# First head's key projected ahead of its query, ScalarE issuing two kinds of stores, and the merge's first loads in four buffers at a fixed place

## The chip, the cores and the metric

The kernel runs on one core of a Trainium2 chip. The metric is the device time of one execution in microseconds; the median of three runs of the kernel before is 1483.13 us (1480.83 to 1486.48).

## What is computed

One step of one layer of a streaming encoder, on 1024 new frames (the prompt) and 32 further frames of a running stream (the samples), T = 1056 tokens of D = 1024 channels. Cut to what matters here:

```python
u = rmsnorm(x) @ w_in               # gq gk gv gr gg | dq dk dv dg | ma mb
dq, dk = rope(dq, pos), rope(dk, pos)
o_gla  = gla(gq, gk, gv, log_a)                     # 4 heads, chunks of 64
o_diff = softmax(q1 k1) v - lam * softmax(q2 k2) v  # 8 heads, two halves of 64 each
yg = rmsnorm(o_gla) * silu(gg)
yd = rmsnorm(o_diff) * (1 - lambda_init) * silu(dg)
merged = sigmoid(ma) * (yg @ w_proj_gla) + sigmoid(mb) * (yd @ w_proj_diff)
return x + rmsnorm(merged @ w_out)                  # and new k, new v, new states
```

## The kernel before

**Numbers.** Everything is fp32. A product is made of three matmuls on split operands: high part of the weights by high part of the data, low by high, high by low (`wh`, `wl`; `X` holds both parts of the data). So every operand of TensorE is first split by ScalarE (the rounded copy) and VectorE or GpSimd (the rest).

**Stages.** Norm and value projections (to about 222 us), the four GLA heads (to 560), differential attention with its eight heads (to 1182), the merge: the projection `pg` of yg (to about 1286), `pd` of yd, `w_out`, and the end. The change is in attention and at the start of the merge.

**How the order is made.** TensorE's order is written out by a planner, `class Order`. Several threads (generators) give steps with a cost, with events that they need and a latency after each (table `W`), and with the PSUM banks that they take. At each moment the first thread whose step is ready by the planner's clock goes: ahead of all the attention heads (`diff_main`), then the samples (`sample_thread`), then `fill`. Fill is a list of projection jobs, in the order of `jobs`. One job is 72 matmuls of 128 x 352: three chunks of 352 tokens, each 8 slices of the channels by 3 products. TensorE runs exactly this list (`tc.manual_schedule(engines=PE)`). The order of the other engines is made by the framework's scheduler, which sees the same program; each engine, SP with its DMA issues included, then works in order, and an instruction that waits holds what is behind it.

**Jobs of attention.** For head h there are `dq h`, `dk h` and `dg h` (the silu gate), and between them 16 gate jobs `g` for the merge, whose tanh is stored to DRAM (`thd`, L484). Before: dq 0, g, dk 0, g, dq 1, g, dk 1, dg 0, dq 2, g, dk 2, dg 1, and so on.

**From a dk job to the scores.** ScalarE evacuates the three chunks to `rr` (L806). SP issues four small DMAs that swap rows for the rope (`sw`, L798 and L799); GpSimd multiplies `sw` by a sine table (L800), VectorE multiplies `rr` by a cosine table (L802, three pieces) and adds (L804). Then ScalarE makes `k0` and `k1` in eight pieces (L833, L834) and VectorE the rests `kl0` and `kl1` (L835, L836). Each of the four tiles is needed in both halves of the partitions, so SP issues four DMAs that copy one half to the other (L839), after a store of the new keys (L827). The scores of a block are two pairs of matmuls: `k0` and `kl0` with `q0`, then `k1` and `kl1` with `q1` (L883, L884); the planner lets them start at the end of the job dk plus `W["dk"]` = 14.32 us, and of dq plus `W["dq"]` = 7.76 us. A dq job has the rope too, and splits into `q0` and `q1` without the copies across halves (L813 to L818). There is one set of `k` and `kl` tiles for all heads.

**The end of a head.** The last scores, transposes (L931) and PV products (L944 to L946) of a head are followed by the first scores of the next, and only then by `diff_fin` of the old head: the sums of squares by `ones` (L859), their store `msd` (L862), the gating of `osb` on VectorE (L865) and its store `ydd` (L866).

**The merge.** `load_split` issues the loads of the eight `ygr` tiles (L1066) into three buffers, each split by ScalarE (L1069) and VectorE (L1070) to `y`. `pg_first` runs two output blocks together, slice by slice as the tiles come; the loads of its weights (`wtile`, L429, one buffer `wr` for the raw weights) and of the stored gates `tha` (L1078) are issued where the scheduler puts them.

Of the kernel before, what the change touches and what calls it, by code (L numbers as in the profile page):

```python
# [11 lines left out]
F32 = mybir.dt.float32  # L12
F32R = mybir.dt.float32r
I32 = mybir.dt.int32
AF = mybir.ActivationFunctionType
ALU = mybir.AluOpType
# [4 lines left out]
P = 128  # L21
NP = 1024
NS = 32
T = NP + NS
D = 1024
KT = D // P
PAST = 512
GH, GDV = 4, 256
DH, HD = 8, 64
# [10 lines left out]
BLK_GQ, BLK_GK, BLK_GG, BLK_DQ, BLK_DK, BLK_DG, BLK_MA, BLK_MB = 0, 4, 8, 16, 24, 32, 40, 48  # L40
BLK_PG, BLK_PD = 56, 64
# [81 lines left out]
def hybrid_step_kernel(ctx: ExitStack, tc: tile.TileContext, a):  # L123
    nc = tc.nc
    mm = nc.tensor.matmul
    act = nc.scalar.activation
    ve = nc.vector
    dma = nc.sync.dma_start
    st = nc.sync.dma_start

    def pool(name, bufs=1, **kw):
        return tc.alloc_tile_pool(name=name, bufs=bufs, **kw)
# [296 lines left out]
    def wtile(b):  # L429
        wr = wp.tile([P, KT, P], F32, tag="wr", bufs=1, name="wr")  # L430
        dma(wr, a["w128"][b])
        wh = odd(wp, KT, P, tag="wh", name="wh")
        act(wh, wr, AF.Copy)  # L433
        wl = odd(wp, KT, P, tag="wl", name="wl")
        nc.gpsimd.tensor_tensor(wl, wr, wh.bitcast(F32), op=ALU.subtract)  # L435
        return wh, wl
# [44 lines left out]
    def gate_job(b, w, j):  # L481
        def begin():
            th = rp.tile([P, T], F32, tag="gate", name="gate")
            return (lambda ps, sl: act(th[:, sl], ps, AF.Tanh, scale=0.5)), (lambda: st(thd[w, j], th))  # L484
        return b, ("gate", w, j), begin, []


# [259 lines left out]
    jobs = []  # L747
# [43 lines left out]
    def rot_job(b, event, needs, split):  # L791
        def begin():
            r = dp.tile([P, T], F32, tag="rr", name="rr")

            def done():
                for m in range(2):
                    o = m * HD
                    dma(sw[o : o + 8], r[o + 8 : o + 16])  # L798
                    dma(sw[o + 8 : o + 16], r[o : o + 8])  # L799
                nc.gpsimd.tensor_tensor(sw, sw, stb, op=ALU.mult)  # L800
                for c in parts(T, N["rr"]):
                    ve.tensor_tensor(r[:, c], r[:, c], ct[:, c], op=ALU.mult)  # L802
                for c in parts(T, N["rr"]):
                    ve.tensor_tensor(r[:, c], r[:, c], sw[:, c], op=ALU.add)  # L804
                split(r)
            return (lambda ps, sl: act(r[:, sl], ps, AF.Copy)), done  # L806
        return b, event, begin, needs

    def split_q(h):
        def f(r):  # L810
            q0 = dp.tile([P, NP], F32R, tag=f"q0{h % 2}", name="q0")
            q1 = dp.tile([P, NP], F32R, tag=f"q1{h % 2}", name="q1")
            for c in parts(NP, N["q"]):  # L813
                act(q0[0:64, c], r[0:64, c], AF.Copy, scale=SC)
                act(q1[64:128, c], r[64:128, c], AF.Copy, scale=SC)
                ve.scalar_tensor_tensor(q0[64:128, c], r[0:64, c], SC, q0[0:64, c].bitcast(F32),
                                        op0=ALU.mult, op1=ALU.subtract)
                ve.scalar_tensor_tensor(q1[0:64, c], r[64:128, c], SC, q1[64:128, c].bitcast(F32),  # L818
                                        op0=ALU.mult, op1=ALU.subtract)
            qsam[h] = sam(0, h)  # L820
            act(qsam[h], r[:, NP:T], AF.Copy, scale=SC)
            dqs[h] = q0, q1
        return f

    def split_k(h):
        def f(r):
            st(a["newk"][h], r)  # L827
            k0 = dp.tile([P, NP], F32R, tag="k0", name="k0")
            k1 = dp.tile([P, NP], F32R, tag="k1", name="k1")
            kl0 = dp.tile([P, NP], F32R, tag="kl0", name="kl0")  # L830
            kl1 = dp.tile([P, NP], F32R, tag="kl1", name="kl1")
            for c in parts(NP, N["k"]):
                act(k0[0:64, c], r[0:64, c], AF.Copy)  # L833
                act(k1[64:128, c], r[64:128, c], AF.Copy)  # L834
                ve.tensor_tensor(kl0[0:64, c], r[0:64, c], k0[0:64, c].bitcast(F32), op=ALU.subtract)  # L835
                ve.tensor_tensor(kl1[64:128, c], r[64:128, c], k1[64:128, c].bitcast(F32), op=ALU.subtract)  # L836

            for t, src, dst in ((k0, 0, 64), (k1, 64, 0), (kl0, 0, 64), (kl1, 64, 0)):
                dma(t[dst : dst + 64].bitcast(F32), t[src : src + 64].bitcast(F32))  # L839
            ksam[h] = sam(1, h)  # L840
            act(ksam[h], r[:, NP:T], AF.Copy)
            dks[h] = (k0, k1), (kl0, kl1)
        return f

    def dgate_job(h):
# [6 lines left out]
            return silu_into(dsg[h]), done  # L852
        return BLK_DG + h, ("dg", h), begin, [(("fin", h - 1), 0.0)] if h else []

    def diff_fin(h, osb, sqo):
        for n0 in (0, 512):
            yield 0.86, [(("pv", h, 3), W["pv"])], ["o"]
            ps = obank("ps_m")
            mm(ps, one_h, sqo[:, n0 : n0 + 512], start=True, stop=True)  # L859
            act(sqo[0:1, n0 : n0 + 512], ps[0:1], AF.Copy)  # L860
            S.free("o", W["m_o"])
        st(msd[h : h + 1, :], sqo[0:1, :])  # L862
        yield 0.0, [(("dg", h), 0.0)], []
        for c in parts(NP, N["fin"]):
            ve.scalar_tensor_tensor(osb[:, c], osb[:, c], gs_half, dsg[h][:, c], op0=ALU.mult, op1=ALU.mult)  # L865
        st(ydd[h, :, 0:NP], osb)  # L866
        S.mark(("fin", h))

    def diff_scores(h, i, out):
# [168 lines left out]
    for h in range(-1, DH):  # L1038
        need = [(("qk", h - 1), 0.0)] if h >= 1 else []
        n = GATES_DIFF[h + 1]  # L1040
        if h + 1 < DH:
            jobs.append(rot_job(BLK_DQ + h + 1, ("dq", h + 1), need, split_q(h + 1)))
        jobs += [gate_job(*gates.pop(0)) for _ in range(min(n, 1))]
        if h + 1 < DH:
            jobs.append(rot_job(BLK_DK + h + 1, ("dk", h + 1), need, split_k(h + 1)))
        if h >= 0:
            jobs.append(dgate_job(h))
        jobs += [gate_job(*gates.pop(0)) for _ in range(n - 1)]
# [9 lines left out]
    lp_ = pool("ldp", reuse_waits="tile")  # L1058

    def ld(name):  # L1060
        return lp_.tile([P, T], F32, tag="ld", bufs=3, name=name)

    def load_split(src, dst, stage, scale=lambda k, r: None):
        for k in range(KT):
            r = stage(k)
            dma(r, src[k])  # L1066
            scale(k, r)
            y = dst[k]
            act(y[:, 0, :], r, AF.Copy)  # L1069
            ve.tensor_tensor(y[:, 1, :], r, y[:, 0, :].bitcast(F32), op=ALU.subtract)  # L1070

    load_split(ygd, ytiles, lambda k: ld("ygr"))
    tha = {}

    def load_tha(j):
        if j < KT:
            tha[j] = ld("tha")
            dma(tha[j], thd[0, j])  # L1078
# [5 lines left out]

    def pg_first():

        w = [wtile(BLK_PG + j) for j in range(2)]
        for j in range(2):
            load_tha(j)
        b = []  # L1090
        for j, k in sorted(((j, k) for j in range(2) for k in range(KT)), key=lambda e: (e[1] + N["lead"] * e[0], e[0])):
            yield 1.36, [(("qk", DH - 1), W["yg0"] + W["yg"] * k)], [] if b else ["pj", "pj", "s", "s"]
            if not b:
                d = [dbank("ps_w") for _ in range(2)]
                b = [bank("ps_w"), bank("ps_w")] + [d[n // 2][:, n % 2 * 512 : n % 2 * 512 + 512] for n in range(4)]
            wh, wl = w[j]
            for n, (t0, cw) in enumerate(CHUNKS):
                ps = b[j * 3 + n]
                mm(ps[:, :cw], wh[:, k, :], ytiles[k][:, 0, t0 : t0 + cw], start=(k == 0), stop=False)
                mm(ps[:, :cw], wl[:, k, :], ytiles[k][:, 0, t0 : t0 + cw], start=False, stop=False)  # L1100
                mm(ps[:, :cw], wh[:, k, :], ytiles[k][:, 1, t0 : t0 + cw], start=False, stop=(k == KT - 1))
            if k == KT - 1:
                with tc.high_priority(offset=N["evac"]):
                    for n, (t0, cw) in enumerate(CHUNKS):
                        pg_evac(j)(b[j * 3 + n][:, :cw], slice(t0, t0 + cw))
                st(ptd[j], tha[j])
                load_tha(j + 2)
                for tag in ("pj", "pj") if j == 0 else ("s", "s"):
                    S.free(tag, W["pg_b"])
        yield from fill([pg_job(j) for j in range(2, KT)], ytiles)  # L1110

    def pg_job(j):
# [4 lines left out]
            return pg_evac(j), done  # L1117
        return BLK_PG + j, ("pg", j), begin, []

    with tc.manual_schedule(engines=PE):  # L1120
        S.run(left + [[pg_first(), None, nullcontext]])
    tp.release()
    rp.release()
    cp = pool("cp", side="right", reuse_waits="tile")
# [176 lines left out]
```

## Time and profile before

| | |
|---|---|
| median of 3 runs | 1483.13 us (1480.83 to 1486.48) |
| the profiled execution | 1483.59 us, its span 1481.9 us |
| TensorE busy | 1422.6 us (96%) |
| VectorE, ScalarE, GpSimd busy | 786.6, 601.0, 298.4 us |
| attention with its fill (560 to 1182 us) | 622 us, TensorE busy 604.9 |
| start of the merge (1182 to 1290 us) | 108 us, TensorE busy 102.5 |

The page gives the span, then each engine's busy time with its share and its number of instructions. The waits view lists who waited for whom: total in us, how often, the longest. The timeline has one row for each instruction or for several of a kind: start, duration, engine, line, what it writes and reads, and in brackets the idle time before it and what ended it. The chain of waits goes back from the last instruction and shows DMAs with the time to their landing. In windows, PEclk is the clock that TensorE was granted, 1.00 being full speed. A matmul's duration overlaps with the next one's, so its cost is the distance between two starts.

### The profile page before, as it was taken

The page shows a single profiled execution, that of the slowest core. Times are in us where ns is not written, and L with a number is a line of the kernel's source. Part 1 is how long each engine was busy: PE and PEld are TensorE (multiplying, and loading weights), DVE is VectorE, ACT ScalarE, POOL GpSimd, SP SyncE. Part 2 cuts the span into 40 slices and gives each one's busy share as a digit, 9 for nine tenths or more (in the row PEclk, how much of TensorE's full clock was granted, in tenths as well). Part 3 has the DMA queues.
Part 4 walks back from the last instruction along what each step waited for, and adds up shares of the span by engine and source line. Part 5 has one row for each costly group of instructions (what it writes and reads, how often), then busy time and mean ns, then how long its engine had stood idle before and what let it go on. Part 6 is the DMA issues. An engine that isn't in the chain of part 4 may idle for free.

```text
span 1481.9 us, 22365 instructions
## 1 busy us (share of the span) xinstructions
PE 1422.6 (96%) x8848; PEld 1327.6 (90%) x8848; DVE 786.6 (53%) x1464; ACT 601.0 (41%) x1262; POOL 298.4 (20%) x186
## 2 busy tenths in 40 slices
PE   8999999989999999899999999999899899999997
PEld 6787789889989899899989998998899799999997
DVE  5702005755565343576767767678665535455415
ACT  5612114535344232455555555555455432221311
POOL 1200002222213224123222222222221111122001
PEclk9999999999999999999999999999999999999999
DMA  8621111122222233323232333223322278633205
GB/s 310 205 105 38 45 45 48 56 74 68 81 70 73 70 120 108 90 62 106 72 108 60 106 86 96 69 83 90 92 68 81 97 264 302 223 131 129 103 1 192
DMA packets 66742, 156.58 MB, mean 106 GB/s; under 512 B 10008, under 2 KB 28568, under 8 KB 65600
## 3 DMA queue, kind: packets, MB, share of 16 engines
q1 hardware_dynamic: 66624, 155.01, 32.3%
q8 instruction: 74, 1.21, 0.3%
q14 instruction: 44, 0.36, 0.1%
HBM read 104.39 MB, written 40.04 MB: 97 GB/s over the span
## 4 chain that ended last, share of the span: by engine, by line
PE 51%; DVE 6%; DMA 4%; ACT 2%; issue 1%; POOL 1%; SPq 0%; DVEq 0%; POOLq 0%; ACTq 0%
PE ps_w L465 9%; PE ps_w L466 9%; PE ps_w L467 9%; PE ps_w L444 2%; PE ps_w L443 2%; PE ps_w L445 2%; PE ps_s L884 2%; PE ps_t L931 2%; PE ps_s L883 2%; DMA ydr<-ydd 2%; PE ps_c L1193 2%; PE ps_c L1195 2%; PE ps_c L1194 2%; PE po L945 1%; PE po L946 1%
## 5 line engine op out<-in xcount | busy, mean ns | idle before, releaser
L465 PE MATMUL ps_w<-X,wh 128*128 128x352 f32 x1344 | 453.8, 338 | 8.5 <-DVE sg L478 3.2
L466 PE MATMUL ps_w<-X,wl 128*128 128x352 f32 x1344 | 438.2, 326 | 0.0
L467 PE MATMUL ps_w<-X,wh 128*128 128x352 f32 x1344 | 436.4, 325 | 0.0
L435 POOL TENSOR_TENSOR wl<-wr,wh 128x1024 fp32r<-128x1024 f32 x72 | 179.5, 2493 | 661.8 <-ACT wh L433 528.6
L465 PEld LDWEIGHTS ps_w<-X,wh 128*128 128x128 f32 x1344 | 255.8, 190 | 13.6 <-issue 4.9
L466 PEld LDWEIGHTS ps_w<-X,wl 128*128 128x128 f32 x1344 | 256.1, 191 | 1.2 <-issue 1.2
L467 PEld LDWEIGHTS ps_w<-X,wh 128*128 128x128 f32 x1344 | 255.1, 190 | 0.0
L889 ACT ACTIVATE p<-ps_s,nm 128x256 f32<-128x256 f32 (+7 forms) x128 | 94.6, 741 | 59.1 <-DVE ps_s L885 31.1
L286 PE MATMUL ps_v<-wh,X 128*128 128x512 f32 x248 | 97.6, 393 | 0.6 <-DVE X L225 0.6
L287 PE MATMUL ps_v<-wl,X 128*128 128x512 f32 x248 | 98.0, 395 | 0.0
L433 ACT ACTIVATE wh<-wr 128x1024 fp32r<-128x1024 f32 x72 | 75.9, 1054 | 54.6 <-PE ps_w L467 30.4
L285 PE MATMUL ps_v<-wh,X 128*128 128x512 f32 x248 | 97.9, 395 | 0.0
L887 DVE TENSOR_REDUCE nm<-ps_s 128x1 f32<-128x256 f32 (+7 forms) x128 | 94.8, 747 | 2.7
L272 DVE TENSOR_TENSOR vo<-ps_v,vo 32x512 f32<-32x512 f32 x4 | 2.7, 679 | 139.9 <-ACT vo L271 139.9
L885 DVE MEMSET ps_s<- 64x64 f32 x128 | 14.3, 112 | 115.8 <-PE ps_s L884 114.2
L650 POOL TENSOR_TENSOR vl<-vr,vh 128x512 fp32r<-128x512 f32 (+1 forms) x20 | 24.8, 1242 | 222.8 <-DVE t L516 160.3
L883 PE MATMUL ps_s<-k,q 128*128 128x512 f32 (+2 forms) x192 | 68.0, 362 | 1.2 <-DMA k<-k 1.2
L884 PE MATMUL ps_s<-kl,q 128*128 128x512 f32 (+2 forms) x192 | 63.8, 348 | 3.9 <-DMA kl<-kl 3.4
L268 ACT ACTIVATE vo<-ps_v 128x512 f32<-128x512 f32 x32 | 19.1, 596 | 114.2 <-PE ps_v L287 113.8
L933 ACT ACTIVATE ah<-ps_t 128x512 fp32r<-128x512 f32 (+2 forms) x96 | 46.9, 488 | 43.6 <-PE ps_t L931 43.0
L934 DVE TENSOR_TENSOR al<-ps_t,ah 128x512 fp32r<-128x512 f32 (+2 forms) x96 | 53.1, 554 | 18.6 <-ACT ah L933 17.3
L444 PE MATMUL ps_w<-Y,wl 128*128 128x352 f32 x192 | 62.2, 324 | 0.0
(319 smaller groups left out, 2960.9 us busy)
## 6 DMA issues: line engine op xcount, KB each, us to landing
wr<-w SPq DMA_DIRECT2D x72, 512.0 KB
thd<-gate SPq DMA_DIRECT2D x16, 528.0 KB
xn<-xn SPq DMA_DIRECT2D x16, 512.0 KB
wr<-wv SPq DMA_DIRECT2D x16, 512.0 KB
newk<-rr SPq DMA_DIRECT2D x8, 528.0 KB
ygr<-ygd SPq DMA_DIRECT2D x8, 528.0 KB
tha<-thd SPq DMA_DIRECT2D x8, 528.0 KB
ydr<-ydd SPq DMA_DIRECT2D x8, 528.0 KB
```

Of the source, the lines that this page charges most:

```text
L285: mm(ps, xk[:, 0, t0 : t0 + P], wh[:, k, :], start=(k == 0), stop=False)
L286: mm(ps, xk[:, 1, t0 : t0 + P], wh[:, k, :], start=False, stop=False)
L287: mm(ps, xk[:, 0, t0 : t0 + P], wl[:, k, :], start=False, stop=(k == KT - 1))
L435: nc.gpsimd.tensor_tensor(wl, wr, wh.bitcast(F32), op=ALU.subtract)
L444: mm(ps[:, :n], wl[:, k, :], src[k][:, 0, t0 : t0 + n], start=False, stop=False)
L465: mm(ps[:, :n], wh[:, k, :], src[k][:, 0, t0 : t0 + n], start=(k == 0), stop=False)
L466: mm(ps[:, :n], wl[:, k, :], src[k][:, 0, t0 : t0 + n], start=False, stop=False)
L467: mm(ps[:, :n], wh[:, k, :], src[k][:, 1, t0 : t0 + n], start=False, stop=(k == KT - 1))
L883: mm(ps[:, n0 : n0 + n], qs[m][:, qsl], ks[m][:, n0 : n0 + n], start=True, stop=False)
L884: mm(ps[:, n0 : n0 + n], qs[m][:, qsl], kls[m][:, n0 : n0 + n], start=False, stop=True)
L887: ve.tensor_reduce(nm, ps[:, 0:w], axis=AX.X, op=ALU.max, negate=True)
L889: act(p[:, 0:w], ps[:, 0:w], AF.Exp, bias=nm, accum_out=sm[:, m : m + 1])
```

## The change

Three things, in one diff.

1. For the first head alone the two jobs change places: dk 0, g, dq 0, g, dq 1, g, dk 1, dg 0, and so on. The planner's tables stay as they are.
2. The stores of the gates (`thd`, 16 of them, 528 KB each) and of the sums of squares (`msd`, 8) are issued by ScalarE, not by SP.
3. The pool of the merge's loads has four buffers and not three. SP's order around these loads is given by hand: the weights of block 0, three ygr loads, the weights of block 1, the other ygr loads, two gates. The store `ydd` of the last head comes behind the planned part of the merge.

```diff
+    sta = nc.scalar.dma_start
...
-            return (lambda ps, sl: act(th[:, sl], ps, AF.Tanh, scale=0.5)), (lambda: st(thd[w, j], th))
+            return (lambda ps, sl: act(th[:, sl], ps, AF.Tanh, scale=0.5)), (lambda: sta(thd[w, j], th))
...
-        st(msd[h : h + 1, :], sqo[0:1, :])
+        sta(msd[h : h + 1, :], sqo[0:1, :])
...
-        st(ydd[h, :, 0:NP], osb)
+        if h < DH - 1:
+            st(ydd[h, :, 0:NP], osb)
+        else:
+            osb_last.append(osb)
...
+        pair = []
         if h + 1 < DH:
-            jobs.append(rot_job(BLK_DQ + h + 1, ("dq", h + 1), need, split_q(h + 1)))
+            pair = [rot_job(BLK_DQ + h + 1, ("dq", h + 1), need, split_q(h + 1)),
+                    rot_job(BLK_DK + h + 1, ("dk", h + 1), need, split_k(h + 1))]
+        if h < 0:
+
+            pair.reverse()
+        jobs += pair[:1]
         jobs += [gate_job(*gates.pop(0)) for _ in range(min(n, 1))]
-        if h + 1 < DH:
-            jobs.append(rot_job(BLK_DK + h + 1, ("dk", h + 1), need, split_k(h + 1)))
+        jobs += pair[1:]
...
-        return lp_.tile([P, T], F32, tag="ld", bufs=3, name=name)
+        return lp_.tile([P, T], F32, tag="ld", bufs=4, name=name)
...
-    load_split(ygd, ytiles, lambda k: ld("ygr"))
...
-        w = [wtile(BLK_PG + j) for j in range(2)]
-        for j in range(2):
-            load_tha(j)
-        b = []
+        w, b = pw, []
...
+    with tc.manual_schedule(engines={E.SP}):
+        pw = [wtile(BLK_PG)]
+        for k in range(3):
+            yg_load(k)
+        pw.append(wtile(BLK_PG + 1))
+        yg_load(3)
+        for k in range(KT):
+            y = ytiles[k]
+            act(y[:, 0, :], yl[k], AF.Copy)
+            ve.tensor_tensor(y[:, 1, :], yl[k], y[:, 0, :].bitcast(F32), op=ALU.subtract)
+            if k + 4 < KT:
+                yg_load(k + 4)
+        for j in range(2):
+            load_tha(j)
     with tc.manual_schedule(engines=PE):
         S.run(left + [[pg_first(), None, nullcontext]])
+    st(ydd[DH - 1, :, 0:NP], osb_last[0])
```

With the first pair exchanged the planner makes another order for the whole of attention. TensorE, where the first scores of head 2 stand (L883 and L884 before, L889 and L890 after). Before, they come in the second chunk (`ps_w_8416`) of the job dq 3, whose weights are `wh_8193`:

```order
L945 MATMUL po_8429<-al_8283,vh_7740 128x128
L946 MATMUL po_8429<-ah_8282,vl_7741 128x128
L883 MATMUL ps_s_8457<-k0_8166,q0_7797 128x128
L884 MATMUL ps_s_8457<-kl0_8168,q0_7797 128x128
L883 MATMUL ps_s_8465<-k1_8167,q1_7798 128x128
L884 MATMUL ps_s_8465<-kl1_8169,q1_7798 128x128
L465 MATMUL ps_w_8416<-X6_88,wh_8193 128x352
L466 MATMUL ps_w_8416<-X6_88,wl_8195 128x352
```

After, they come ahead of the first matmul of dq 3, whose weights are `wh_8252` there:

```order
L951 MATMUL po_8359<-al_8192,vh_7694 128x128
L952 MATMUL po_8359<-ah_8191,vl_7695 128x128
L889 MATMUL ps_s_8387<-k0_8225,q0_7831 128x128
L890 MATMUL ps_s_8387<-kl0_8227,q0_7831 128x128
L889 MATMUL ps_s_8395<-k1_8226,q1_7832 128x128
L890 MATMUL ps_s_8395<-kl1_8228,q1_7832 128x128
L466 MATMUL ps_w_8413<-X6_88,wh_8252 128x352
L467 MATMUL ps_w_8413<-X6_88,wl_8254 128x352
```

So between the last matmul of the job dk 2 and these scores stood the 72 matmuls of dg 1 and 36 of dq 3, and now stand the 72 of dg 1 alone. Counted in the same way for heads 0 to 7, the fill matmuls between the end of dk and the first scores are 96, 108, 108, 102, 102, 114, 114, 108 before, and 198, 72, 72, 78, 72, 78, 72, 78 after. From the end of dq 0 to the first scores of head 0 they are 240 before and 54 after.

SP, the same boundary: the store of the new keys of head 2 (`newk`), the copies across halves, and the store of the gated output of head 1 (`ydd<-osb`). Before:

```order
L827 DMA newk<-rr_7962 128x1056
L839 DMA k0_8166<-k0_8166 64x1024
L839 DMA k1_8167<-k1_8167 64x1024
L839 DMA kl0_8168<-kl0_8168 64x1024
L839 DMA kl1_8169<-kl1_8169 64x1024
L968 DMA vcs_8377<-cachev 128x4x128
L968 DMA vcs_8384<-cachev 128x4x128
L431 DMA wr_8600<-w128 128x1024
L909 DMA vr_9295<-newv 128x8x128
L866 DMA ydd_83<-osb_7744 128x1024
```

After:

```order
L828 DMA newk<-rr_8040 128x1056
L840 DMA k0_8225<-k0_8225 64x1024
L840 DMA k1_8226<-k1_8226 64x1024
L840 DMA kl0_8227<-kl0_8227 64x1024
L870 DMA ydd_83<-osb_7698 128x1024
L840 DMA kl1_8228<-kl1_8228 64x1024
L432 DMA wr_8591<-w128 128x1024
L915 DMA vr_9233<-newv 128x8x128
```

The store has moved from five places behind the last copy to one place ahead of it. So it is for heads 1, 2, 4 and 6; for heads 3, 5 and 7 it stands right behind the copies. On VectorE the gating of `osb` (L868 after) now stands there between the last piece of `kl1` and the first scores' `ps_s`, where it stood behind those scores.

SP at the start of the merge, after:

```order
L432 DMA wr_13061<-w128 128x1024
L974 DMA vcs_12916<-cachev 128x4x128
L974 DMA vcs_12923<-cachev 128x4x128
L1131 DMA ygr_13067<-ygd_82 128x1056
L1131 DMA ygr_13069<-ygd_82 128x1056
L1131 DMA ygr_13071<-ygd_82 128x1056
L432 DMA wr_13073<-w128 128x1024
L1131 DMA ygr_13079<-ygd_82 128x1056
```

Before, the weights of blocks 0, 1 and 2 stood ahead of all ygr loads, and behind the first two of these came the last head's `ydd`.

More of the change, by code (lines that the diff above doesn't have):

```diff
@@ L853, in dgate_job @@
         return BLK_DG + h, ("dg", h), begin, [(("fin", h - 1), 0.0)] if h else []
+    osb_last = []
     def diff_fin(h, osb, sqo):
@@ L1118, in pg_job, with yg_load @@
         return BLK_PG + j, ("pg", j), begin, []
+    yl = {}
+    def yg_load(k):
+        yl[k] = ld("ygr")
+        dma(yl[k], ygd[k])
+    with tc.manual_schedule(engines={E.SP}):
[12 more added lines that the diff above has]
+            load_tha(j)
     with tc.manual_schedule(engines=PE):
         S.run(left + [[pg_first(), None, nullcontext]])
+    st(ydd[DH - 1, :, 0:NP], osb_last[0])
     tp.release()
```

## The prediction

> **What bounds the kernel now.** I read the page's head first, then TensorE's list of waits, then its idle gaps stretch by stretch.
>
> ```profile
> span 1481.9 us, 22365 instructions
> PE 1422.6 (96%) x8848; PEld 1327.6 (90%) x8848; DVE 786.6 (53%) x1464; ACT 601.0 (41%) x1262; POOL 298.4 (20%) x186
> ```
>
> TensorE is busy for 1422.6 of 1481.9 us. No other engine comes near, and the change alters no matmul, so it can only move TensorE's 59 us of idle time, add to it, or change the clock. The waits view (total, times, longest) says what ended that idle time in the stages that the change touches:
>
> ```profile
> PE ps_t L931 <- DVE al L934: 4.1, 3, 1.4
> ...
> PE ps_st L1006 <- DVE smp L1009: 3.6, 2, 2.3
> PE ps_s L884 <- DMA kl<-kl: 3.4, 3, 2.2
> ...
> PE ps_t L931 <- DVE smp L1032: 1.7, 1, 1.7
> PE ps_w L1101 <- DVE y L1070: 1.6, 2, 0.9
> PE ps_w L1099 <- ACT y L1069: 1.5, 1, 1.5
> ...
> PE ps_so L1029 <- DVE al L934: 1.2, 2, 0.7
> PE ps_s L883 <- DMA k<-k: 1.2, 1, 1.2
> ```
>
> Three kinds can be had: the scores' wait for k and kl (4.6), waits around the sample rows and the last transposes (4.1 + 3.6 + 1.7 + 1.2 = 10.6, of which 1.41 belongs to the end of attention), and the merge's first waits (3.1). That is about 18 us, so no edit here gains much more than 1%.
>
> **First head.** The scores of head 0 follow dk 0 directly. Rows of its chain, from the timeline and the chain of waits:
>
> ```profile
> 583.69 0.47 ACT L806 ACTIVATE rr<-ps_w 128x352 f32<-128x352 f32 x1 [3.40 <-PE ps_w L467]
> 588.76 2.82 POOL L800 TENSOR_TENSOR sw<-sw,stb 128x1056 f32<-128x1056 f32 x1 [1.18 <-DMA sw<-rr]
> 588.73 3.67 DVE L802 TENSOR_TENSOR rr<-rr,ct 128x352 f32<-128x352 f32 x3 [12.78 <-DMA sw<-rr]
> 592.32 1.39 DVE L804 TENSOR_TENSOR rr<-rr,sw 128x352 f32<-128x352 f32 x3
> 597.55 0.42 DVE L836 TENSOR_TENSOR kl<-rr,k 64x256 fp32r<-64x256 f32 x1
> 598.35 1.64 SPq L839 DMA_DIRECT2D kl<-kl  x2
> 598.35 4.27 DMA kl<-kl
> 602.76 0.46 PE ps_s L884
> 604.72 0.29 PE ps_w L466
> ```
>
> From the evacuation of the job's last chunk (583.69) it takes 5.1 us until the rope's swaps have landed, 5.0 for the rope, 4.3 for the pieces of k and kl (the last ends at 597.97, 14.3 after the start) and 4.8 for the swap across partition halves: kl is complete 19.1 us after the job. The planner counts on W["dk"] = 14.32, which is the end of the last piece and leaves the swap out. TensorE lost 1.16 + 2.20 + 0.45 = 3.8 us here, and then more by its clock:
>
> ```profile
> core 0: us, PE busy (x) PEld busy (x) DVE busy (x) ACT busy (x) POOL busy (x), PEclk, DMA share, GB/s
> ...
> 604.00:608.00 4.00, 4.00 (x14) 4.00 (x15) 1.27 (x5) 0.68 (x4) 0.00 (x0) 0.50 0.12 46
> 608.00:612.00 4.00, 4.00 (x24) 4.00 (x24) 0.12 (x2) 0.47 (x1) 0.00 (x0) 0.86 0.00 0
> 612.00:616.00 4.00, 4.00 (x27) 4.00 (x26) 2.05 (x7) 2.46 (x7) 0.00 (x0) 1.00 0.00 0
> ```
>
> At a granted clock of 0.50 and 0.86 the 8 us after the stall did 2.0 + 0.56 us less work; not all of the first 4 us was at half speed, so I take 2.2 us. (Matmuls start 0.29 us apart there, as at 604.72, where 0.16 is usual.) The stall with its tail costs 6.0 us. After the change dk 0 is three jobs old by then, and dq 0 comes last: the first scores stand 54 fill matmuls, 8.7 us, after it. The query has no swap across halves: 5.1 for the rope's swaps, 5.0 for the rope and about 1 us for the first pieces (an estimate, from the 0.42 of a kl piece half as wide) make 11.1 us. A stall of 2.4 us is left, with about 1 us of clock: **gain 2.5** (0 to 6).
>
> **The other heads: what the earlier start does.** This is where I expect the time to go. How much cover the k chain has before the change is seen in stretches from the last evacuation of dk to the head's first scores (heads 1, 3, 6), counting only the first of each three fill matmuls:
>
> ```profile
> core 0: us, PE busy (x) PEld busy (x), PEclk, DMA share, GB/s
> ...
> 648.18:673.86 25.68, 11.85 (x36) 6.58 (x35) 1.00 0.39 103
> ...
> 792.88:817.58 24.70, 11.33 (x34) 6.31 (x34) 1.00 0.34 93
> ...
> 1004.70:1034.09 29.39, 12.39 (x37) 6.92 (x37) 1.00 0.38 99
> ```
>
> There the scores come 102 to 111 fill matmuls and 25 to 29 us after the job, so the missing swap in W["dk"] never showed: before, the planner was held by attention's own work, which had started late because dk 0 was last. With dk 0 ahead the first scores come 42 fill matmuls earlier, all of attention moves up against the fill, and now the planner's term for dk decides at every head. In the new order the scores of heads 1, 2, 4 and 6 stand exactly one job (72 fill matmuls) after dk, those of 3, 5 and 7 78. What that is in time:
>
> ```profile
> 592.01 0.16 PE ps_w L466
> ...
> 799.87 0.44 PE ps_t L931 x4
> ...
> 795.79 0.28 PE L944 MATMUL po<-ah,vh 128*128 128x256 f32 x1
> ...
> 797.72 0.27 PE L946 MATMUL po<-ah,vl 128*128 128x128 f32 x1
> ```
>
> 72 x 0.161 = 11.6, the 24 matmuls of the last PV at 0.114 (17 steps from 795.79 to 797.72) = 2.7, and 11 transposes at 0.11 = 1.2: 15.6 us; for heads 3, 5 and 7 about 17.1. The chain needs at least 19.1, as at head 0, where nothing competed. At head 3 it took longer:
>
> ```profile
> 813.83 4.78 DMA kl<-kl
> ...
> 818.66 0.33 PE ps_s L884
> ...
> 819.31 2.97 DVE L865 SCALAR_TENSOR_TENSOR osb<-osb,gs_half,sg 128x1024 f32<-128x1024 f32 x1
> ...
> 822.31 0.33 SPq L866 DMA_DIRECT2D ydd<-osb  x1
> ```
>
> kl landed at 818.6, 25.8 after 792.88, behind the softmax of the last query block on VectorE. After the change that softmax is mostly over when the rope begins, so I stay near the lower row and add 2 us for the silu, al and gate pieces that VectorE and ScalarE still have in between: kl0 lands about 21 us after dk. In heads 1, 2, 4 and 6 there is a second step. SP's new order puts ydd <- osb of the old head between the swap of kl0 and that of kl1; in the row above it was issued long after both. It waits for osb on VectorE, which needs the last PV (15.6), vh, the square and the copy on ScalarE (about 2 us), and then 1.3 us alone or up to the 2.97 above: osb is ready at 19 to 20.8, and kl1 is issued behind it and lands 4.3 to 4.8 us later, at about 24.5. Behind the store and kl1 on SP stands the next wr load; no wait of TensorE before names a late wr, so I count nothing for it.
>
> - Heads 1, 2, 4, 6: 24.5 - 15.6 - 0.5 (the scores themselves) = 8.4 us of stall each, 33.6.
> - Heads 3, 5, 7: kl1 at 22, 22 - 17.1 - 0.5 = 4.4 each, 13.2.
> - Clock behind seven stalls at least as long as head 0's: 7 x 2.2 = 15.4.
>
> The bounds: at best every chain ends after 19.1 and SP's new order costs nothing (4 x 3.5 + 3 x 2 = 20, clock 7 x 1); at worst 25.8, and 3 us more behind osb (4 x 12.7 + 3 x 8.2 = 75, clock 17.5).
>
> The Trainium skill's page "DMA: Bandwidth & Descriptors" (Anatomy of one DMA) gives a fixed 2.0 us plus bytes over 436 GB/s, which for a 256 KB swap would be an estimated 2.6 us; the swaps of kl here took 4.27 and 4.78, so the rows decide; by the page each of the seven stalls would be 1.7 us shorter (3.4 with kl1 queued behind the store's wait, if that is shortened too), 12 to 19 us in all.
>
> The page "TensorE: Matmul & The Clock Gate" (Part 1) has the clock at half after an idle window of about 3.4 us and full again after about 3.4 us of work. The row at 604 agrees with the size (0.50 for about 4 us after gaps of 3.8 us in all); by the page a stall costs an estimated 1.7 us of clock and the shorter ones may cost none, so the term of 15.4 would be 7 to 12.
>
> **Sample rows, last transposes.** Their steps move against the rest. In the new order the second transposes of the samples stand further behind the first ones, with scores and fill between. The waits there come to the 10.6 us above less 1.4 at the end of attention, 9.2, and the clock lost 0.4 + 1.3 us after one of them:
>
> ```profile
> 1036.00:1040.00 4.00, 1.69 (x6) 0.89 (x6) 3.81 (x6) 1.82 (x8) 1.68 (x1) 0.90 0.27 70
> 1040.00:1044.00 4.00, 4.00 (x16) 3.52 (x16) 0.16 (x1) 0.11 (x1) 0.00 (x0) 0.67 0.52 192
> ```
>
> I take 7 of these 9.2 + 1.7 = 10.9 us as **gained** (3 to 11).
>
> **Merge.** Fill now lasts to the end of attention, and the first ygr loads go out before the gates' and the last ydd store. But ScalarE still has the last square, copy and gate ahead of y0, so part of the 1.5 + 1.6 us stays: **gain 3** (1 to 6). The later tha loads and the moved ydd store are hidden by the eight slices of the first two blocks and by the blocks behind them: 0; without that cover, 2 us.
>
> **Stores from ScalarE.** 24 issues at about 0.33 us (the row of ydd above is such an issue, by SP) are 8 us on an engine busy for 41%. Each waits for ScalarE's own last piece, so nothing else is held: 0, at worst 2. SP loses its waits for gates:
>
> ```profile
> SPq L484 <- ACT gate L484: 89.8, 14, 10.6
> ```
>
> Nothing of TensorE's waits leads back to them, so this gains 0.
>
> **Sum.** 1483.6 (the profiled execution; 1.7 of it outside its span, and 0.5 above the median) + 46.8 + 15.4 - 2.5 - 7 - 3 = 1533.3: **1533 us**.
>
> **Rivals.** (1) Faster: the chain at the boundaries shortens to under 16 us, since the engines have less queued there, and the seven stalls vanish. Then the gains alone remain: 1483.6 - 12.5 = 1471; with all of the 18.3 us of waits gone and the clock's 2.2 + 1.7 with them, 1461. The point that decides is kl's landing 15.6 to 17.1 us after dk. For it: at heads 1 to 7 now the chain is stretched by other work. Against: head 0's row has 19.1 with VectorE free, and its parts are fixed durations. 11%. (2) No change: kl lands some 2 us after the scores' place, so that the stalls stay too short to touch the clock and eat the gains: 7 x 1.8 = 12.6, 1483. Between 19.1 and 15.6 only a shorter swap gives this. 7%. (3) Worse than forecast: the 25.8 of head 3 holds at all heads, and osb comes on top: 1483.6 + 75 + 17.5 - 8 = 1568. 22%. (4) The second step does not happen, since osb is early or the store is let through: all heads stall about 4.5: 31.5 + 14 - 12.5, 1517. 20%. My forecast has 40%.
>
> **Chances and range.** 0.5% (7.4 us) is about what a measurement of this kernel can tell from no change. Low end: the best bound with gains of 17: 1483.6 + 20 + 7 - 17 = 1494. High end: rival 3, 1568. Outside lie rivals 1 and 2 and a little above. Faster 0.11, same 0.07, slower 0.82.
>
> **What would show it.** Right: TensorE's waits for kl and k grow from 4.6 us to about 45, at seven places, with kl's landing about 21 to 25 us after the evacuation; the clock falls below 0.7 after each; in heads 1, 2, 4 and 6 the wait for the second kl is the longer one, with the swap's issue right behind ydd's. Wrong: if the scores of heads 1 to 7 wait under 2 us, the chain is shorter than any row of before shows it, or the order runs otherwise. If the waits are there and the clock stays at 1.00, only its term fails.

## The result, and the profile after

The changed kernel takes 1548.47 us (median of 6 runs, 1543.36 to 1556.19) against 1483.99 us for the kernel before (6 runs). The ratio is 1.0436, with a 95% interval of 1.0403 to 1.0469: slower by 64.5 us. The profiled execution took 1547.3 us, 1545.6 of it in its span. The ratios below leave out one execution of a later run, of 3013.65 us (the run with both latencies raised, one of five).

The page's head of the changed kernel, to be held against 1481.9 and 1422.6 before:

```profile
span 1545.6 us, 22331 instructions
...
PE 1442.6 (93%) x8848; PEld 1342.5 (87%) x8848; DVE 779.9 (50%) x1464; ACT 598.4 (39%) x1262; POOL 311.2 (20%) x186
```

The number of matmuls is the same. The span grew by 63.7 us: TensorE's idle time from 59.3 to 103.0 us (+43.7), and its busy time by 20.0, which with the same work means a slower clock (the mean granted clock is 0.972 where it was 0.990). So two terms carry the whole loss, and both were in the prediction's sum. TensorE's waits (total, times, longest):

```profile
PE ps_s L890 <- DMA kl<-kl: 27.4, 11, 3.3
PE ps_s L889 <- ACT osb L954: 11.1, 5, 3.1
PE ps_t L937 <- DVE al L940: 6.5, 6, 1.8
PE ps_s L889 <- DMA k<-k: 5.6, 2, 3.2
PE ps_s L889 <- DVE q L817: 5.2, 1, 5.2
PE ps_st L1012 <- DVE al L940: 4.4, 3, 1.5
...
PE ps_w L1106 <- ACT y L1141: 1.9, 1, 1.9
```

The waits of the first scores for k and kl were 4.6 us before. Now the lines for kl, k and `osb`, with 1.2 us behind `nm`, make 45.3 us, at seven places. One head start of each kind, from TensorE's timeline (head 4, with the store `ydd` between the two copies of kl, and head 5, with the store behind them):

```profile
919.73 0.30 PE L889 MATMUL ps_s<-k,q 128*128 128x128 f32 x1 [3.13 <-ACT osb L954]
922.08 0.45 PE L890 MATMUL ps_s<-kl,q 128*128 128x128 f32 x1 [2.06 <-DMA kl<-kl]
926.01 0.44 PE L890 MATMUL ps_s<-kl,q 128*128 128x128 f32 x1 [3.27 <-DMA kl<-kl]
...
1004.04 0.30 PE L889 MATMUL ps_s<-k,q 128*128 128x128 f32 x1 [1.65 <-ACT osb L954]
1006.47 0.44 PE L890 MATMUL ps_s<-kl,q 128*128 128x128 f32 x1 [2.13 <-DMA kl<-kl]
1007.51 0.44 PE L890 MATMUL ps_s<-kl,q 128*128 128x128 f32 x1 [0.39 <-DVE nm L893]
```

Three waits follow each other at head 4: k, then kl0, then kl1, 8.46 us; at head 5 the third has shrunk to 0.39 (the row puts it down to `nm`) and 4.17 us are left in all. The first wait is put down to `osb`, which is no operand of these scores: it seems that ScalarE's copy merely ended at about the time when k landed. In the run where `osb`'s store was moved (below) the same wait, 3.15 us long, is put down to `k<-k`. Head 2 shows the chain, first SP's issues, then ScalarE and VectorE, then the chain of waits:

```profile
753.56 1.16 SPq L840 DMA_DIRECT2D k<-k  x2
754.82 0.58 SPq L840 DMA_DIRECT2D kl<-kl  x1
758.75 0.34 SPq L870 DMA_DIRECT2D ydd<-osb  x1
759.19 0.46 SPq L840 DMA_DIRECT2D kl<-kl  x1
```

```profile
738.97 0.47 ACT L807 ACTIVATE rr<-ps_w 128x352 f32<-128x352 f32 x1
...
756.29 0.37 ACT L954 ACTIVATE osb<-po 128x256 f32<-128x256 f32 x1
```

```profile
756.70 2.03 DVE L868 SCALAR_TENSOR_TENSOR osb<-osb,gs_half,sg 128x1024 f32<-128x1024 f32 x1 [1.78 <-ACT osb L954]
```

```profile
759.19 3.73 DMA kl<-kl
763.06 0.44 PE ps_s L890
```

From the last evacuation of dk 2 (738.97) the second kl takes 24.0 us (763.0; the prediction had 24.5). SP issues the copy of kl1 3.8 us after that of kl0 was done issuing, behind the store that waits for `osb`. And the clock around it:

```profile
core 0: us, PE busy (x) PEld busy (x) DVE busy (x) ACT busy (x) POOL busy (x), PEclk, DMA share, GB/s
752.00:756.00 4.00, 1.67 (x16) 1.53 (x14) 2.76 (x7) 3.88 (x8) 1.08 (x2) 1.00 0.62 183
756.00:760.00 4.00, 0.86 (x3) 0.68 (x3) 2.07 (x2) 0.66 (x3) 4.00 (x2) 0.62 0.59 177
760.00:764.00 4.00, 1.03 (x5) 0.97 (x5) 0.74 (x4) 0.46 (x2) 0.93 (x1) 0.50 0.99 293
764.00:768.00 4.00, 4.00 (x14) 3.52 (x14) 0.89 (x4) 0.46 (x2) 0.00 (x0) 0.60 0.42 122
768.00:772.00 4.00, 4.00 (x25) 3.52 (x24) 0.66 (x4) 1.80 (x4) 0.00 (x0) 1.00 0.02 4
```

After the stall 14 fill matmuls start in 4 us where 25 do at full clock.

### The profile page after: what moved, and what is told of

Its sections match the earlier page's. It is cut to its first block, busy times and chain, and to the rows that moved or that the text cites. A ratio compares the mean times of both kernels' runs of the same rounds, so it can differ in the third digit from the quotient of the medians.

```text
span 1545.6 us, 22331 instructions
## 1 busy us (share of the span) xinstructions
PE 1442.6 (93%) x8848; PEld 1342.5 (87%) x8848; DVE 779.9 (50%) x1464; ACT 598.4 (39%) x1262; POOL 311.2 (20%) x186
## 4 chain that ended last, share of the span: by engine, by line
PE 49%; DVE 8%; DMA 4%; ACT 3%; issue 2%; POOL 1%; SPq 0%; DVEq 0%; POOLq 0%; ACTq 0%
PE ps_w L466 9%; PE ps_w L467 8%; PE ps_w L468 8%; DMA kl<-kl 2%; PE ps_s L890 2%; PE ps_w L445 2%; PE ps_w L444 2%; PE ps_w L446 2%; PE ps_c L1221 2%; PE ps_c L1223 2%; PE ps_c L1222 2%; PE ps_s L889 2%; PE ps_t L937 2%; PE ps_m L862 1%; DVE p L900 1%
## 5 line engine op out<-in xcount | busy, mean ns | idle before, releaser
L466 PE MATMUL ps_w<-X,wh 128*128 128x352 f32 x1344 | 461.2, 343 | 8.6 <-DVE sg L479 3.2
L468 PE MATMUL ps_w<-X,wh 128*128 128x352 f32 x1344 | 440.4, 328 | 0.0
L466 PEld LDWEIGHTS ps_w<-X,wh 128*128 128x128 f32 x1344 | 259.6, 193 | 16.5 <-issue 7.0
L467 PEld LDWEIGHTS ps_w<-X,wl 128*128 128x128 f32 x1344 | 259.3, 193 | 3.0 <-issue 2.9
L468 PEld LDWEIGHTS ps_w<-X,wh 128*128 128x128 f32 x1344 | 258.2, 192 | 0.2 <-issue 0.2
L890 PE MATMUL ps_s<-kl,q 128*128 128x512 f32 (+2 forms) x192 | 66.4, 360 | 28.6 <-DMA kl<-kl 27.4
L889 PE MATMUL ps_s<-k,q 128*128 128x512 f32 (+2 forms) x192 | 69.7, 369 | 22.0 <-ACT osb L954 11.1
L890 PEld LDWEIGHTS ps_s<-kl,q 128*128 128x128 f32 x192 | 37.9, 197 | 35.6 <-DVE osb L868 15.6
L900 DVE SCALAR_TENSOR_TENSOR p<-p,sm 128x128 f32<-128x128 f32 (+3 forms) x64 | 67.3, 1052 | 2.0
```

The costliest lines, as they stand in the source:

```text
L466: mm(ps[:, :n], wh[:, k, :], src[k][:, 0, t0 : t0 + n], start=(k == 0), stop=False)
L467: mm(ps[:, :n], wl[:, k, :], src[k][:, 0, t0 : t0 + n], start=False, stop=False)
L468: mm(ps[:, :n], wh[:, k, :], src[k][:, 1, t0 : t0 + n], start=False, stop=(k == KT - 1))
L889: mm(ps[:, n0 : n0 + n], qs[m][:, qsl], ks[m][:, n0 : n0 + n], start=True, stop=False)
L890: mm(ps[:, n0 : n0 + n], qs[m][:, qsl], kls[m][:, n0 : n0 + n], start=False, stop=True)
L900: ve.scalar_tensor_tensor(pt[0][:, 0:w], pt[0][:, 0:w], sm[:, 0:1], pt[1][:, 0:w], op0=ALU.mult, op1=ALU.add)
```

## The experiments

Theory A is the prediction's: the exchange of the first pair lets the planner's short latency for dk decide at every head. Theory B puts the loss to the stores on ScalarE and the merge's order. C and the others are named where they come up. Where not said otherwise the edit is made to the changed kernel.

**The exchange alone** (made to the kernel before).

```diff
+        if h < 0:
+            pair.reverse()
```

> The kernel before with the first pair of jobs exchanged and nothing else. If the exchange alone lets the planner's 14.32 us for dk decide at every head (theory A), this is about as slow as the whole change: seven waits for kl of 4 to 8.5 us, clock tails behind each, and none of the merge's gain, 1545 to 1555 us. If the stores issued by ScalarE or the order of SP at the merge cause the loss (theory B), it stays within 1475 to 1490 us.

Measured: 1550.77 us, ratio 1.0459 (1.0432 to 1.0487). The exchange alone gives the whole loss; its waits for kl (27.3 us) and k read like those above. Theory B falls as the cause of the 64.5 us.

**All but the exchange.**

```diff
-        if h < 0:
-
-            pair.reverse()
```

> The changed kernel without the exchange: ScalarE's stores and the merge's loads alone. Theory A: the first scores stand where they stood before, the waits for kl are those of before (about 4.6 us), and only the merge's gain is left: 1476 to 1484 us. Theory B: 1520 us or more.

Measured: 1488.76 us, 1.0025 (1.0012 to 1.0037). Theory A holds for the large part, but there is a small loss and not the merge's gain that I had expected; the last three runs below take it apart.

**The planner's latency for dk at 20 us.**

```diff
-"dk": 14.32,
+"dk": 20.0,
```

> The changed kernel with the planner's latency for dk raised from 14.32 to 20.0 us and nothing else; the first scores of heads 1 to 7 then stand 102 to 114 fill matmuls after dk, as in the kernel before. Theory A: waits for kl under 2 us in all from head 1 on, no clock tails there; head 0 keeps its wait for q (about 5 us): 1478 to 1488 us. Theory B: unchanged at 1540 us or more.

Measured: 1493.13 us, 1.0063 (1.0044 to 1.0082). One number of the planner takes back 55 of the 64.5 us. On TensorE's timeline no head start from 2 on waits more than 0.6 us; head 0 still waits 4.63 us for q, head 1 1.42 for kl. It is 5 us above the expected range: its trace also has the waits that the stores bring by themselves (the last runs below), 1.55 + 0.34 us at 1000 us and 3.65 at 1079.

**Both latencies at what the traces show.**

```diff
-"dq": 7.76, "dk": 14.32,
+"dq": 14.0, "dk": 26.0,
```

> The changed kernel with the latencies for dk and dq at what the traces show, 26 and 14 us in place of 14.32 and 7.76. Theory A: no head waits for k, kl or q for over 1 us, so all stalls of both kernels at the heads' starts go, and the merge's gain stays: 1470 to 1480 us. Theory B: 1535 us or more.

Measured: 1501.98 us, 1.0105 (1.0079 to 1.013). Missed: it should have been the best. All waits for q, k and kl are gone, but attention starts later against the fill, and the sample rows' steps then stand where nothing covers them:

```profile
PE ps_t L937 <- DVE smp L1038: 10.1, 3, 3.4
PE ps_st L1012 <- DVE smp L1015: 7.9, 4, 2.3
PE ps_t L937 <- DVE al L940: 5.6, 4, 1.7
```

Before, the first two lines were 1.7 and 3.6. A latency that is right for one thread moved the others.

**The store `ydd` issued by ScalarE**, so that SP's copy of kl1 follows that of kl0; theory C has kl1 late for another reason.

```diff
         if h < DH - 1:
-            st(ydd[h, :, 0:NP], osb)
+            sta(ydd[h, :, 0:NP], osb)
```

> The changed kernel with the store ydd of heads 0 to 6 issued by ScalarE, so that on SP the copy of kl1 follows that of kl0 at every head; TensorE's order is the same. If the store's place is the second step of the stall (theory A), the wait of about 3 us before the second pair of scores goes at heads 1, 2, 4 and 6 and they look like heads 3, 5 and 7: 4 x 4 us less idle, 1530 to 1536 us. If kl1 is late for another reason (its pieces, the landing itself; theory C), no change: 1545 to 1551 us.

Measured: 1538.05 us, 1.0358 (1.0337 to 1.0378), 10.4 us less than the changed kernel and 2 us above the range expected. Head 4 again:

```profile
913.05 0.30 PE L889 MATMUL ps_s<-k,q 128*128 128x128 f32 x1 [3.15 <-DMA k<-k]
915.49 0.44 PE L890 MATMUL ps_s<-kl,q 128*128 128x128 f32 x1 [2.15 <-DMA kl<-kl]
916.63 0.44 PE L890 MATMUL ps_s<-kl,q 128*128 128x128 f32 x1 [0.48 <-DMA kl<-kl]
```

The third wait falls from 3.27 to 0.48 us, so the store's place made it; theory C falls. I had counted 4 us for each of four heads; the stalls of these heads now add up to 22.6 us in place of 32.9, which is nearly the 10.4.

**Matmuls of no use in the stall**, for the clock. First dose:

```diff
+            if i == 0 and h > 0:
+                for _ in range((9, 6)[m] if h in (1, 2, 4, 6) else (7, 0)[m]):
+                    mm(ps[:, 0:512], one_h, xs[0][:, 0, 0:512].bitcast(F32), start=True, stop=True)
```

> The changed kernel with matmuls of no use (128x512, fp32, 9 and 6 of them at heads 1, 2, 4, 6; 7 at heads 3, 5, 7) ahead of the first scores, a little shorter than the stalls, written to the bank that the scores then overwrite. The stalls stay as long, but TensorE works through most of them. If the slower clock behind a stall comes from the idle time, the tails go: 7 x 2.3 us, 1530 to 1536 us. If the tails have another cause, 1546 to 1552 us.

Measured: 1555.9 us, 1.0481 (1.046 to 1.0501). Inconclusive in time: one of these fp32 matmuls took 0.77 us and not the 0.43 that I had taken, so the dose was longer than the stall it should fill (9 of them ran 6.9 us at head 1, against 4.4 of wait). The clock stayed at 1.00 at all seven places. Second dose, (5, 3) and (4, 0):

> The run with matmuls of no use again, with 5 and 3 of them at heads 1, 2, 4, 6 and 4 at heads 3, 5, 7, since one took 0.77 us there and the first dose (11.7 and 5.7 us for each head) was longer than the stalls of 7.5 to 8.5 and 4.2. Now 3.9 + 2.3 and 3.1 us, shorter than the stalls. If idle time makes the slow clock: granted clock 1.00 behind each head's start and 1532 to 1537 us. If not: clock still 0.5 to 0.9 there, 1545 to 1550 us.

Measured: 1532.96 us, 1.0313 (1.0289 to 1.0338): 15.5 us less than the changed kernel, with 44 needless matmuls more. Head 2 there:

```profile
752.00:756.00 4.00, 3.65 (x10) 1.52 (x8) 2.18 (x3) 2.25 (x4) 3.17 (x2) 1.00 0.80 197
756.00:760.00 4.00, 2.98 (x8) 1.36 (x8) 0.71 (x3) 0.46 (x2) 2.52 (x1) 1.00 0.73 201
760.00:764.00 4.00, 3.38 (x18) 2.94 (x19) 1.27 (x5) 0.67 (x3) 0.00 (x0) 1.00 0.81 264
764.00:768.00 4.00, 4.00 (x25) 3.52 (x24) 1.00 (x5) 1.94 (x5) 0.00 (x0) 1.00 0.00 1
```

PEclk (third column from the right) is 1.00 where it was 0.62, 0.50, 0.60, and the wait for k and kl is as long as ever, only worked through. So the clock's tails (the slow time behind a stall) are made by the idle time, and they are worth some 15.5 us.

**The small loss: stores on ScalarE alone** (made to the kernel before, all 24).

```diff
-            ... st(thd[w, j], th)
+            ... sta(thd[w, j], th)
-        st(msd[h : h + 1, :], sqo[0:1, :])
+        sta(msd[h : h + 1, :], sqo[0:1, :])
```

> The kernel before with the stores of gates and means issued by ScalarE, and nothing else. If the loss of 0.25% without the exchange comes from these stores (they hold ScalarE or shift the scheduler's order, as the waits at 996 and 1074 us there suggest): 1486 to 1491 us. If it comes from the merge's order: 1482 to 1485 us.

Measured: 1492.59 us, 1.0066 (1.0041 to 1.0091). **The merge's part alone** (to the kernel before):

```diff
+    with tc.manual_schedule(engines={E.SP}):
+        pw = [wtile(BLK_PG)]
...
```

> The kernel before with the merge's loads in four buffers in SP's order by hand and the last store moved, and nothing else. If the stores cause the loss of 0.25% without the exchange: 1479 to 1484 us, since two of the merge's waits are shorter. If the merge's order causes it: 1486 to 1491 us.

Measured: 1482.35 us, 0.9992 (0.9978 to 1.0005), no difference. So the stores lose, the merge's order neither gains nor loses by itself. Beside the stores it does gain: with both, but without the exchange, the ratio was 1.0025 (1.0012 to 1.0037), with the stores alone 1.0066 (1.0041 to 1.0091), and the merge's first wait for y is 1.51 us there and 3.38 here. **The 16 stores of the gates alone**, and then **the 8 small ones alone** (to the kernel before, one line each of the diff above):

> The kernel before with the 16 stores of the gates issued by ScalarE and the 8 small ones left to SP. If a collision of a shifted VectorE instruction with GpSimd (as at 988 us with both kinds moved) and the reordering around the gates cause that run's loss: 1488 to 1494 us again. If the means' stores cause it: 1482 to 1485 us.

Measured: 1483.14 us, 0.9992 (0.998 to 1.0004).

> The kernel before with the 8 stores of the sums of squares issued by ScalarE and the 16 of the gates left to SP. With both kinds moved the time was 1492.6 us, with the gates' alone 1483.1. If the small stores alone bring the collision of VectorE's q piece with GpSimd near 988 us and the later ScalarE row at the merge: 1488 to 1494 us. If it takes both kinds together: 1481 to 1486 us.

Measured: 1490.76 us, 1.0054 (1.0035 to 1.0072). The eight stores of 4 KB cost some 7 us; the sixteen of 528 KB nothing. The traces point to the order: without their place on SP the scheduler sets VectorE's pieces around head 6's dq otherwise. Before, the last piece of q (0.69 us) was done ahead of GpSimd's split of the next weights (VectorE, then GpSimd):

```profile
987.15 0.69 DVE L818 SCALAR_TENSOR_TENSOR q<-rr,q 64x512 fp32r<-64x512 f32 x1
```

```profile
988.04 2.86 POOL L435 TENSOR_TENSOR wl<-wr,wh 128x1024 fp32r<-128x1024 f32 x1 [9.28 <-ACT wh L433]
```

With the eight stores alone on ScalarE it comes behind the scaling of p, and into GpSimd's instruction (VectorE, GpSimd, TensorE):

```profile
986.68 2.82 DVE L819 SCALAR_TENSOR_TENSOR q<-rr,q 64x512 fp32r<-64x512 f32 x1
```

```profile
986.45 2.50 POOL L436 TENSOR_TENSOR wl<-wr,wh 128x1024 fp32r<-128x1024 f32 x1 [9.41 <-PE ps_s L885]
```

```profile
992.02 0.39 PE L945 MATMUL po<-ah,vh 128*128 128x256 f32 x1 [1.58 <-ACT ah L934]
```

0.69 us become 2.82, the next scores' `nm` comes later by that, and TensorE waits 1.58 + 0.33 us for the copies of the transposes that depend on it, with a clock of 0.58 in the 4 us behind. From the wait for `al` at 914.23 to the one at 1030.08, with this place between them, TensorE takes 3.8 us longer than before (915.97 to 1027.99). In this run, as in the two others without the exchange that have these eight stores on ScalarE, the wait of the sample rows near 1070 us is 3.64 to 3.66 us long where it was 1.66; from there to the end of attention it takes 1.7 us more. Another 1.4 lie in the merge (the wait for `tha` grew from 1.8 to 3.7 us). That the changed order is the cause is read from these rows; no run put the order back by itself.

**A version meant to be best**: exchange and merge's order, no stores on ScalarE, latencies of 20 us (dk) and 13 us (dq).

> The exchange and the merge's loads, without ScalarE's stores, with the planner's latencies at 20 us for dk and 13 us for dq. The first scores of head 0 stand 90 fill matmuls after dq 0 (14.5 us), those of heads 1 to 7 102 to 114 after dk. Theory A: no wait for q or k over 0.5 us at head 0, at most 1.5 us at the others, so head 0's 6 us are gained: 1473 to 1480 us. If the sample rows or the end of attention give it back: 1481 to 1486 us.

Measured: 1490.55 us, 1.0035 (1.0021 to 1.005). Missed. Head 0's wait falls to 1.65 us, but kl of head 7 makes TensorE wait 1.8 us, and the end of attention and the merge's start run at clocks down to 0.50. No version that ran beats the kernel before.

## Why the prediction was right, point by point

1. **What bounds the kernel, and where the loss comes from: right, and shown.** The exchange alone gives the loss, one planner's latency takes most of it back.
2. **Stalls of heads 1, 2, 4, 6 at 8.4 us and of 3, 5, 7 at 4.4 us: right.** Measured 7.53, 8.44, 8.46, 8.42 and 4.16, 4.17, 4.19, in all 45.4 where the sum had 46.8. Rival 4 (store let through) and rival 3 (the 25.8 us of head 3 at all heads) did not come. At heads 1, 2, 4 and 6 the parts came as forecast: the scores of kl0 20.2 to 20.5 us after the evacuation (21 expected), those of kl1 24.0 to 24.1 (24.5), with TensorE ready for them after 14.7 to 15.5 (15.6). At heads 3, 5 and 7 there is luck in it: the scores of kl1 began 23.7 us after the evacuation, where kl1 was expected at 22, and TensorE had come to the first scores after 18.5, where 17.1 were expected; the two misses cancel. The prediction's estimate of 2.6 us for a copy, from the Trainium skill's page "DMA: Bandwidth & Descriptors" (Anatomy of one DMA), takes a fit that the page gives for DMAs issued by GpSimd. SP issues these copies, and they landed after 3.73 to 4.78 us; no term of the sum rests on the 2.6.
3. **Clock, 7 x 2.2 = 15.4: right.** The filled stalls give back 15.5. The Trainium skill's page "TensorE: Matmul & The Clock Gate" (Part 1), by which the term would have been 7 to 12, fits the mechanism (idle time gates, work releases) and is too small here: the short stalls of heads 3, 5 and 7, 4.2 us broken up by single score matmuls, slow the clock as long as the long ones (0.50 and 0.88 in the two slices from 1008 behind head 5; 0.60 and 1.00 in the two from 764 behind head 2).
4. **Head 0, gain 2.5: wrong, the step failed.** Two of its terms were too small. The first is the clock. With the exchange alone the chain of the query is what was forecast: 11.3 us from the last evacuation (583.84) to the end of the first piece that VectorE makes of q, where 11.1 were expected, and a wait of 2.74 + 0.20 us where 2.4 were. But the clock behind it was 0.50 in the slice from 596 and 0.72 in the next, about 3 us less work (an estimate from these two slices) where 1 was put. That makes the 6.0 us of the kernel before again, and no gain. The second is the rope, counted with 5.0 us as for dk 0. In the whole change it came late (GpSimd's rows, then VectorE's, then TensorE's):

```profile
593.10 2.79 POOL L436 TENSOR_TENSOR wl<-wr,wh 128x1024 fp32r<-128x1024 f32 x1 [7.00 <-ACT wh L434]
595.85 2.40 POOL L801 TENSOR_TENSOR sw<-sw,stb 128x1056 f32<-128x1056 f32 x1
```

```profile
598.28 1.40 DVE L805 TENSOR_TENSOR rr<-rr,sw 128x352 f32<-128x352 f32 x3 [4.64 <-POOL sw L801]
```

```profile
600.68 0.48 PE L889 MATMUL ps_s<-k,q 128*128 128x128 f32 x1 [5.18 <-DVE q L817]
```

   With the exchange alone (GpSimd, then TensorE):

```profile
586.97 2.41 POOL L435 TENSOR_TENSOR wl<-wr,wh 128x1024 fp32r<-128x1024 f32 x1 [6.84 <-ACT wh L433]
589.33 2.75 POOL L800 TENSOR_TENSOR sw<-sw,stb 128x1056 f32<-128x1056 f32 x1
```

```profile
595.21 0.33 PE L883 MATMUL ps_s<-k,q 128*128 128x128 f32 x1 [2.74 <-DVE q L816]
```

   GpSimd splits a weight tile ahead of the multiplication of `sw` in both, as it did in the kernel before (585.18, then 588.76). What differs is when that tile is there: SP issued its load at 586.12 in the whole change and at 580.15 with the exchange alone, each time right after GpSimd had ended the split of the tile before. That split waited for ScalarE's `wh`, which stands behind the evacuation of dq 0's first chunk in the whole change (582.18, then 582.54), and ahead of it with the exchange alone (576.58, then 577.53). The runs with the exchange and the stores on ScalarE have the late order; the version meant to be best, with the merge's order and without these stores, has the early one (578.08, then 579.03). So this part comes with the stores. It makes 5.2 us of wait where 2.4 were expected and 3.8 had been before, with a clock of 0.50 and 0.65 behind it: a loss of about 2 in place of a gain of 2.5. The prediction left out GpSimd's queue, and the weights that it waits for.

5. **Sample rows and last transposes, gain 7: wrong.** 6.5 + 4.4 = 10.9 us of waits are there (the lines for al and `ps_st` above) where 9.2 and a clock tail of 1.7 had been: nothing gained. The steps moved to places with other waits; that they would find cover was never read from an order of VectorE. This is the largest miss of the sum.
6. **Merge, gain 3: about right in size, in part by luck.** The waits for y, 3.1 us before, are still 1.87 + 0.70. The rest of the gain was given no price: the transposes' wait of 1.41 at the end of attention and the clock tail behind the first y (0.75 and 0.83 in the slices from 1184) are gone, and the waits for `tha` in the later blocks fell from 1.8 to 0.9. The loads alone give nothing (0.9992), but beside the exchange they help. Here are the first waits for y with the exchange alone, then in the changed kernel:

```profile
1244.92 0.43 PE L1103 MATMUL ps_w<-y,wh 128*128 128x352 f32 x1 [2.30 <-ACT y L1073]
1247.53 0.66 PE L1105 MATMUL ps_w<-y,wh 128*128 128x352 f32 x1 [2.01 <-DVE y L1074]
```

```profile
1249.23 0.43 PE L1106 MATMUL ps_w<-y,wh 128*128 128x352 f32 x1 [1.87 <-ACT y L1141]
1250.52 0.43 PE L1108 MATMUL ps_w<-y,wh 128*128 128x352 f32 x1 [0.70 <-DVE y L1142]
```

   The clock behind the first pair was 0.65 in the slice from 1248; behind the second it stayed at 1.00.
7. **Stores from ScalarE, 0 to 2 us: wrong by themselves**, 7 to 9 us, though not by holding ScalarE, as the bound had it: the 16 large ones cost nothing there, the 8 small ones cost 7 us. In the changed kernel their cost is hidden in the total: they bring the late rope of head 0 (point 4) and a longer wait at the last GLA head (1.76 us where it was 0.48), and the merge's order takes about as much off (point 6). So the whole change (1.0436) and the exchange alone (1.0459) cannot be told apart.

The sum misses by 14 us of span, of which points 4 and 5 are about 12. Some 2 us lie ahead of the first scores: the evacuation of the first job's last chunk comes at 562.86 us after and 560.53 before, and 1.3 of that is the longer wait at the last GLA head, which every run with the gates' stores on ScalarE shows and no other.

What stays open: why the scheduler sets the order of VectorE and ScalarE otherwise when a store changes its queue, and whether another place for these stores would have avoided it, was not tried.

## What to carry to other kernels

A latency in a planner's table that ends at the last compute instruction, and not where the data have landed, does no harm as long as something else is later; ask of every reordering which such numbers come into force. A latency corrected alone is no cure: here it moved the stall to another thread. And in an order made by a scheduler a store moved to another queue is a change of every engine's order, to be read there before it is called free.

## What the runs showed of the hardware

- A piece of VectorE's with both inputs in SBUF took 2.82 us instead of 0.69 when it began 0.23 us into a GpSimd instruction of 2.50 us; two other runs show 2.79 and 2.80 at the same place. The Trainium skill's page "GPSIMD Engine Reference" (Specifications) has the SBUF interfaces shared, with contention for instructions with two SBUF inputs; the rows agree, and the piece takes longer than all of the GpSimd instruction.
- How long a wait must be to slow the clock is not one length in these runs. The sample rows' wait of 2.31 us was followed by 4 us at 0.57 with the planner's dk at 20 us (first row below), and by 1.00 with the merge's part alone (second row) and in three other runs. 1.58 + 0.33 us were followed by 0.58 with the eight small stores alone, 1.55 + 0.34 by 1.00 with dk at 20 us. 1.4 us did nothing at head 1 of that run. All seven head starts of the changed kernel, 4.2 to 8.5 us long, slowed the clock, at 2.2 us each (15.5 by seven).

```profile
1048.00:1052.00 4.00, 3.79 (x14) 3.80 (x15) 0.88 (x4) 0.21 (x1) 0.00 (x0) 0.57 0.74 256
```

```profile
1040.00:1044.00 4.00, 3.54 (x21) 3.09 (x22) 1.24 (x5) 0.65 (x2) 0.00 (x0) 1.00 0.76 259
```

- The copies of 256 KB across partition halves landed 3.73 us after their issue at the best and 4.78 at the longest of those shown.
